# Two of six down groups of each FFN as seven half-size products, and low parts of weights made by adding transfers

## The chip, the cores and the metric

The kernel runs on one core of a Trainium2 chip. Its engines work side by side, each from its own queue in order: TensorE (PE: matmuls into PSUM, with its weight loads, PEld, beside them), VectorE (DVE), ScalarE (ACT), GpSimd (POOL) and SyncE (SP, which only starts transfers). Sixteen DMA engines move data for all of them. The metric is device microseconds of one execution of the whole program; lower is better.

## The reference

A decoder trunk of two layers on x of 1 x 512 x 1024 in float32. Each layer is a half-step SwiGLU FFN, a mixer (gated linear attention in the first layer, stick-breaking attention in the second), and another half-step FFN; a norm ends the trunk. So there are four FFNs, and they hold most of the work:

```python
def swiglu(h, w_gate, w_up, w_down):
    return (jax.nn.silu(h @ w_gate) * (h @ w_up)) @ w_down
...
for i in range(DEPTH):
    x = x + 0.5 * swiglu(rmsnorm(x, ffn1_norm[i]), ffn1_w_gate[i], ffn1_w_up[i], ffn1_w_down[i])
    h = rmsnorm(x, mix_norm[i])
    ...
    x = x + y.astype(x.dtype)
    x = x + 0.5 * swiglu(rmsnorm(x, ffn2_norm[i]), ffn2_w_gate[i], ffn2_w_up[i], ffn2_w_down[i])
```

The model width is 1024, the hidden width 2816, the sequence 512 tokens.

## The kernel before, in words

**Tiling.** Everything is held transposed: features on the 128 partitions, the 512 tokens along the free dimension. x is eight tiles of 128 x 512 (`xs`). A float32 product is made of three matmuls in a shorter format (`F32R`): each operand is cut into a high part h (the value cast on ACT) and a low part l = value - h (a subtraction on DVE), and the matmuls are h h, l h and h l. `Entry.split` (lines 110 to 135) cuts weights, `FFN.cut` (668) cuts activations.

**Order of the work.** All weight products stand in one list, `feed.q`. An `Entry` has one or two units of weights (a unit is at most 128 x 1024 elements of a loaded chunk, or sums made from it) and a body that issues its matmuls. `Feed.start` (141) begins an entry: it splits the units of this entry and of the next two, as long as they hold at most four full units together, makes the views (the sums) of the next four and loads the chunks of the next six. Four buffers of high and of low parts (`wh`, `wl`) go round, so a unit can be cut when the matmuls of the unit four places earlier are through. Loads are started by SyncE in order, each when its buffer is free: two buffers of 1 MB (`raw`) and two of 512 KB (`rawd`, for down weights). The framework's planner orders each engine's queue from the program's order, its own costs and the dependencies.

**One FFN.** The 11 blocks of 256 hidden features form six groups, `GROUPS = ((0, 2), (2, 4), (4, 6), (6, 8), (8, 9), (9, 11))`. Gate and up of the first two blocks are plain products (`feat`: 24 matmuls of 512 columns each); all others use `seven` (560): the product of a 2 x 2 block matrix by seven products of half size in place of eight (Strassen's scheme in Winograd's form), with 12 matmuls of 256 columns for each. Sums of weights are made on DVE (`sums_12`, `sums_34`), sums of the activations once per FFN (`sums`). A seven is two entries: the first block column and s12 (`body_1`, four products), s34 and a half unit a22 (`body_2`, three products). `gate` and `close` turn the result into hidden tiles (h, l) of 128 x 512.

The down products of a group are `down` entries (297), placed between the sevens of the next group: for a group of two blocks (four hidden tiles) four entries, each with 24 matmuls of 512 columns into two PSUM tiles `ps_d`, which DVE then adds into x (323). The last group's downs end the FFN; in the last FFN `back_tok` takes their place. Where a seven follows an entry whose weights lie at another offset, a copy of its first 128 x 128 weights is made as well (`lead`, 131 to 135).

PSUM has eight banks of 128 x 512 that `psum` hands out in turn.

Of the kernel before, what the change touches and what calls it, by code (L numbers as in the profile page):

```python
# [28 lines left out]
NEAR, NEAR_MOVING = 16, 48  # L29
# [3 lines left out]
def decoder(ctx: ExitStack, tc: tile.TileContext, a: dict, out: bass.AP):  # L33
    nc = tc.nc
# [60 lines left out]
    class Entry:  # L95
# [3 lines left out]

        def __init__(self, units, body, place=0, lead=False):  # L100
            self.units, self.body, self.W, self.place = units, body, None, place
            self.lead, self.views = lead, None

        def view(self):

# [1 line left out]
                self.views = [view(ch.load()) for ch, view, _, _ in self.units]  # L107
            return self.views

        def split(self):  # L110
            if self.W is None:
                self.W = []
                for r, (_, _, n, m) in zip(self.view(), self.units):
                    few = n * m < 1024
                    if few:

                        h = st["few"].tile([P, n * m + NEAR], F32R, tag="vh", bufs=1, name="wh")[:, NEAR:]
                        l = st["few"].tile([P, n * m + 64 - NEAR], F32R, tag="vl", bufs=1, name="wl")[:, : n * m]
                    else:
                        h, l = (  # L120
                            wp.tile([P, n * m + 64], F32R, tag="w" + t, bufs=4, name="w" + t)[
                                :, self.place : self.place + n * m
                            ]
                            for t in "hl"
                        )
                    h, l = (t.rearrange("p (n m) -> p n m", m=m) for t in (h, l))
                    st["cut"] = nc.scalar.copy(h, r).ins  # L127
                    with tc.issue_after(st["gains"]):
                        nc.vector.tensor_tensor(out=l, in0=r, in1=h.bitcast(F32), op=ALU.subtract)  # L129
                    self.W.append((h, l))  # L130
                    if self.lead and len(self.W) == 1:

                        first = wp.tile([P, m], F32R, tag="w1", bufs=1, name="w1")
                        nc.scalar.copy(first, r[:, 0])
                        self.first = first

    class Feed:
# [46 lines left out]
    feed = Feed()  # L184
# [112 lines left out]
    def down(w, r0, nf, hs, part, nxt, late=0):  # L297


        nd = KD // nf  # L300
        src = w[r0 : r0 + nf * P, part * nd * P : (part + 1) * nd * P]
        ch = Chunk(src.rearrange("(f p) c -> p f c", p=P), nf, nd * P)
        ch.few = True

        def body(W):
            (wh, wl), = W
            acc = []

            def prod(m, fs):
                if m == len(acc):  # L310
                    acc.append(psum("ps_d"))
                s = slice(m * P, (m + 1) * P)
                for f in fs:
                    mm3(acc[m], wh[:, f, s], wl[:, f, s], hs[f][0], hs[f][1], f == 0, f == nf - 1)

            if late:
                for m in range(nd):
                    prod(m, range(nf - late))
            for m in range(nd):
                prod(m, range(nf - late if late else 0, nf))  # L320
                ps = acc[m]
                k = part * nd + m
                nc.vector.scalar_tensor_tensor(  # L323
                    out=xs[k], in0=ps, scalar=0.5, in1=xs[k], op0=ALU.mult, op1=ALU.add
                )
                if nxt is not None:
                    nxt(k)
                yield

        feed.q.append(Entry([(ch, lambda t: t, nf, nd * P)], body))  # L330

    def back_tok(w, r0, nf, hs, done):

# [159 lines left out]
    class FFN:  # L493
# [5 lines left out]

        GROUPS = ((0, 2), (2, 4), (4, 6), (6, 8), (8, 9), (9, 11))  # L500
        NORMED, SEVEN, AHEAD = 6, 2, 2
        SEVEN_UP = (2, 3, 4, 5, 6, 7, 8, 9, 10)

        def __init__(self, wg, wu, wd, gi, nxt, first=False, last=False):
            self.gi, self.normed = gi, False
            self.after_ffn = bool(phases) and isinstance(phases[-1], FFN)
            self.defer, self.gates = [], []
            self.lead = []
            self.hs = [[] for _ in self.GROUPS]
            base, downs = len(feed.q), []  # L510
# [48 lines left out]

        def seven(self, ch, group=None):  # L560
# [62 lines left out]
            def body_2(W):  # L623
# [9 lines left out]
                nc.vector.tensor_tensor(out=o0[:, H:T], in0=q, in1=o0[:, H:T], op=ALU.add)  # L633
                gate(o0, H, o0[:, H:T])
                if group is not None:
                    self.close(o0, group)
                gate(o1, H, o1[:, H:T])
                yield
                prod(w, a22, 0, lambda j: self.t_half(3, j), first=False)
                gate(o1, 0, w)  # L640
                if group is not None:
                    self.close(o1, group)
                    del self.gates[:2]
                else:
                    self.gates += [o0, o1]
                yield


            lead = feed.q[-1].place != NEAR
# [70 lines left out]
        def close(self, t, group):  # L720
            h = self.hp.tile([P, T], F32R, tag="hh", name="hh")
            l = self.hp.tile([P, T], F32R, tag="hl", name="hl")
            self.hs[group].append(self.cut(h, l, t))

        def run(self, between=None):
            with tc.tile_pool(name="hp", bufs=8, reuse_waits="tile") as self.hp, tc.tile_pool(
# [712 lines left out]
```

## Time and profile before

| | us |
|---|---|
| median of 3 runs (1855.47 to 1856.14) | 1856.08 |
| the profiled execution | 1854.57 |
| its span, first to last instruction | 1852.6 |
| PE busy in it | 1836.5 (99%) |
| DVE busy | 1421.5 (77%) |
| ACT busy | 1012.7 (55%) |
| POOL busy | 8.8 |
| mean granted TensorE clock | 0.999 |

A group's row gives line, engine, operation, output<-inputs, shape and count, then the busy time in us with the mean ns of one instruction, then the idle time of the engine before them and what ended it. In the table of waits a row says who waited, for whom, the total in us, how often, and the longest. In the chain, a row is start, length and engine with tile and line, xN for N instructions in a row. PE's matmuls overlap, so the duration of one is longer than the distance from one to the next.

### The profile page before, as it was taken

The numbers are of one execution on the slowest core, as the hardware profiler recorded it, in microseconds if no ns is written. First come the engines' busy times: TensorE is split into PE (matmuls) and PEld (weight loads), VectorE is DVE, ScalarE is ACT, GpSimd is POOL, SyncE is SP. The second block draws the span as 40 slices with busy tenths as digits, with TensorE's granted clock in tenths as the row PEclk, the third lists the DMA queues.
The fourth block names the chain that finished last, engine by engine and source line by source line (L and its number), as shares of the span: only waits on it lengthen the run. The fifth ranks groups of instructions, "written<-read, shape, count | busy, mean of one in ns | idle before, by whom it ended". The sixth has DMA issues, their size and how long they took to land.

```text
span 1852.6 us, 29092 instructions
## 1 busy us (share of the span) xinstructions
PE 1836.5 (99%) x11899; PEld 1645.3 (89%) x11899; DVE 1421.5 (77%) x2172; ACT 1012.7 (55%) x1735; POOL 8.8 (0%) x20
## 2 busy tenths in 40 slices
PE   8999999999999999999999999999999999999998
PEld 7999999889888899999889999998878788999997
DVE  7977776776787987777798777676878779877775
ACT  7545545444555554544555545455888755544454
POOL 0000000100000000000000000000000000000000
PEclk9999999999999999999999999999999999999999
DMA  5333333221223233333233333222221123333321
GB/s 160 114 126 114 103 115 102 91 68 48 69 69 114 91 114 108 109 103 102 85 111 114 103 103 114 98 86 80 69 69 61 65 91 97 120 103 110 119 80 69
DMA packets 177610, 179.11 MB, mean 97 GB/s; under 512 B 4099, under 2 KB 167989, under 8 KB 177477
## 3 DMA queue, kind: packets, MB, share of 16 engines
q1 hardware_dynamic: 176768, 176.18, 29.5%
q8 instruction: 93, 1.52, 0.3%
q0 software_dynamic: 608, 1.05, 0.2%
q14 instruction: 41, 0.33, 0.1%
q10 hardware_dynamic: 100, 0.03, 0.0%
HBM read 175.17 MB, written 2.10 MB: 96 GB/s over the span
## 4 chain that ended last, share of the span: by engine, by line
PE 95%; DVE 2%; ACT 2%; DMA 1%; issue 0%; SPq 0%; ACTq 0%; DVEq 0%
PE ps_d L67 25%; PE ps_w L587 21%; PE ps_f L67 18%; PE ps_q L587 10%; PE ps_z L587 5%; PE ps_t L67 5%; PE ps_b L67 4%; PE ps_S L67 1%; PE ps_bt L67 1%; PE ps_z L1163 1%; PE ps_oT L1225 1%; PE ps_T L1210 1%; PE ps_o L67 1%; DMA x<-in_x_dram 1%; ACT wh L127 0%; DVE wl L129 0%
## 5 line engine op out<-in xcount | busy, mean ns | idle before, releaser
L129 DVE TENSOR_TENSOR wl<-raw,wh 128x1024 fp32r<-128x1024 f32 (+1 forms) x244 | 258.8, 1063 | 91.8 <-ACT wh L127 59.7
L127 ACT CAST wh<-raw 128x1024 fp32r<-128x1024 f32 (+1 forms) x244 | 224.8, 923 | 119.3 <-PE ps_d L67 40.1
L67 PE MATMUL ps_d<-hh,wl 128*128 128x512 f32 x672 | 262.1, 390 | 0.0
L67 PE MATMUL ps_d<-hh,wh 128*128 128x512 f32 x672 | 262.1, 390 | 0.0
L67 PE MATMUL ps_d<-hl,wh 128*128 128x512 f32 x672 | 261.4, 389 | 0.0
L587 PE MATMUL ps_w<-th,wh 128*128 128x256 f32 x864 | 238.8, 276 | 0.4 <-ACT ps_z L611 0.4
L587 PE MATMUL ps_w<-tl,wh 128*128 128x256 f32 x864 | 238.6, 276 | 0.0
L587 PE MATMUL ps_w<-th,wl 128*128 128x256 f32 x864 | 238.5, 276 | 0.0
L127 ACT CAST wh<-s 128x1024 fp32r<-128x1024 f32 x144 | 151.1, 1049 | 121.0 <-PE ps_q L587 41.5
L129 DVE TENSOR_TENSOR wl<-s,wh 128x1024 fp32r<-128x1024 f32 x144 | 175.6, 1221 | 51.4 <-PE ps_z L587 28.3
L323 DVE SCALAR_TENSOR_TENSOR x<-ps_d,x 128x512 f32<-128x512 f32 x184 | 124.7, 687 | 101.3 <-PE ps_d L67 100.4
L127 ACT CAST wh<-rawd 128x1024 fp32r<-128x1024 f32 x84 | 88.5, 1055 | 179.7 <-PE ps_d L67 97.3
L67 PE MATMUL ps_f<-xh,wh 128*128 128x512 f32 x448 | 179.0, 400 | 0.0
L67 PE MATMUL ps_f<-xl,wh 128*128 128x512 f32 x448 | 175.7, 392 | 0.0
L67 PE MATMUL ps_f<-xh,wl 128*128 128x512 f32 x448 | 175.1, 391 | 0.0
L587 PEld LDWEIGHTS ps_w<-th,wh 128*128 128x128 f32 x864 | 162.2, 188 | 0.8 <-ACT ps_z L611 0.8
L587 PEld LDWEIGHTS ps_w<-th,wl 128*128 128x128 f32 x864 | 162.2, 188 | 0.0
L587 PEld LDWEIGHTS ps_w<-tl,wh 128*128 128x128 f32 x864 | 162.2, 188 | 0.0
L67 PEld LDWEIGHTS ps_d<-hl,wh 128*128 128x128 f32 x672 | 126.2, 188 | 26.7
L67 PEld LDWEIGHTS ps_d<-hh,wh 128*128 128x128 f32 x672 | 126.1, 188 | 24.7
L67 PEld LDWEIGHTS ps_d<-hh,wl 128*128 128x128 f32 x672 | 126.1, 188 | 24.1
L129 DVE TENSOR_TENSOR wl<-rawd,wh 128x1024 fp32r<-128x1024 f32 x84 | 102.8, 1224 | 52.9 <-ACT wh L127 39.1
(276 smaller groups left out, 4442.2 us busy)
## 6 DMA issues: line engine op xcount, KB each, us to landing
raw<-in_ffn_w_gate_dram SPq DMA_DIRECT2D x43, 1024.0 KB, 5.1
raw<-in_ffn_w_up_dram SPq DMA_DIRECT2D x43, 1024.0 KB, 5.2
rawd<-in_ffn_w_down_dram SPq DMA_DIRECT2D x84, 512.0 KB, 3.5
raw<-in_gla_w_in_dram SPq DMA_DIRECT2D x12, 1024.0 KB, 5.5
raw<-in_sb_w_in_dram SPq DMA_DIRECT2D x16, 512.0 KB, 3.8
raw<-in_gla_w_out_dram SPq DMA_DIRECT2D x4, 1024.0 KB, 4.9
raw<-in_sb_w_in_dram SPq DMA_DIRECT2D x4, 1024.0 KB, 5.3
raw<-in_sb_w_out_dram SPq DMA_DIRECT2D x4, 1024.0 KB, 4.9
```

Of the source, the lines that this page charges most:

```text
L67: st["pe"] = nc.tensor.matmul(ps, l, r, start=first, stop=last).ins
L127: st["cut"] = nc.scalar.copy(h, r).ins
L129: nc.vector.tensor_tensor(out=l, in0=r, in1=h.bitcast(F32), op=ALU.subtract)
L323: nc.vector.scalar_tensor_tensor(out=xs[k], in0=ps, scalar=0.5, in1=xs[k], op0=ALU.mult, op1=ALU.add)
L587: st["pe"] = nc.tensor.matmul(o, l_, r_, start=first and j + n == 0, stop=j == 3 and n == 2, skip_group_check=True).ins
L1163: nc.tensor.matmul(o_, l_, r_, start=first, stop=last, skip_group_check=True)
L1210: nc.tensor.transpose(ps[:, c0 : c0 + P], ys[yb][:, yc + j * P : yc + (j + 1) * P], ident)
L1225: nc.tensor.matmul(po[e * 64 : e * 64 + 64, j * P : T], self.v[j][:, c : c + 64], self.wt[p, e][bk][:, c0 : c0 + n], start=j == 0, stop=j ...
```

## The change

Three things change.

First, the down products of the second and the fourth group (`DOWN_SEVEN = (1, 3)`) are no longer four `down` entries each but two parts of a new function, `seven_down`: the same seven-product scheme with the down weights as the left matrix (two chunks of 512 KB, `lower` and `upper`, in the two `rawd` buffers) and the hidden tiles as the right one. A part makes four of the eight output tiles. It uses six PSUM banks; ACT copies two of them from bank to bank, and each product is added by DVE into half a tile of x as soon as it stands. Part 0 comes after the second seven of the next group, part 1 after the first seven of the group behind that.

Second, the hidden tiles of those groups are closed in another form: `close_first` and `close_second` make the sums of the right matrix (four differences of 128 x 256 on DVE) and cut them and the plain quarters. Their high and low parts lie in the hidden tiles' buffers, in halves of the normed input that no product reads then, and in two tiles of the norm.

Third, the low part of some units is no longer made by a DVE subtraction: ACT writes l = -value in the short format, and GpSimd starts a transfer that adds the loaded value to it. This holds for the first unit of every entry with `adds`: plain `down` entries, sevens that are no `lead`, and the first entry of each `seven_down` part. `Feed.start` gains a rule that splits the first unit of such an entry one entry earlier. As a side effect fewer sevens follow a plain down, so fewer have `lead`.

```diff
@@ class Entry @@
+    def split(self, few=None):
+
         if self.W is None:
             self.W = []
-            for r, (_, _, n, m) in zip(self.view(), self.units):
+        if len(self.W) < len(self.units):
+            for r, (_, _, n, m) in list(zip(self.view(), self.units))[len(self.W) : few]:
...
                 st["cut"] = nc.scalar.copy(h, r).ins
+                if self.adds and len(self.W) == 0:
+
+                    nc.scalar.activation(l, r, AF.Copy, scale=-1.0)
+                    nc.gpsimd.dma_start(out=l, in_=r, accum_op=ALU.add)
+                    self.W.append((h, l))
+                    continue
...
@@ Feed.start @@
             if used > 4:
+
+                if used == 5 and len(e.units) == 2 and e.adds:
+                    e.split(1)
                 break
...
+    def seven_down(pool, w, r0, hs, part):
...
+        H = T // 2
+        lower, upper = (
+            Chunk(w[r0 : r0 + 4 * P, c : c + 256].rearrange("(f p) c -> p f c", p=P), 4, 256)
+            for c in (part * 256, 512 + part * 256)
+        )
+        lower.few = upper.few = True
...
+        def sums_12(_):
+            a11, _, a21, a22 = halves()
+            s = v["s12"] = pool().tile([P, 4, 256], F32, tag="s", bufs=4, name="s12")
+            nc.vector.tensor_tensor(out=s[:, 0:2], in0=a21, in1=a22, op=ALU.add)
+            nc.vector.tensor_tensor(out=s[:, 2:4], in0=s[:, 0:2], in1=a11, op=ALU.subtract)
+            return s
...
+        def prod(ps, w, k0, step, m, b, first):
+            for c in range(2):
+                bh, bl = hs[c][b]
+                wh, wl = (t[:, k0 + step * c, m * P : (m + 1) * P] for t in w)
+                for n, (l_, r_) in enumerate(((wh, bh), (wl, bh), (wh, bl))):
+                    st["pe"] = nc.tensor.matmul(
+                        ps, l_, r_, start=first and c + n == 0, stop=c == 1 and n == 2, skip_group_check=True
+                    ).ins
+
+        def add(m, up, col, ps):
+            x = xs[part * 2 + m + 4 * up][:, col * H : col * H + H]
+            nc.vector.scalar_tensor_tensor(out=x, in0=ps, scalar=0.5, in1=x, op0=ALU.mult, op1=ALU.add)
+
+        def body_1(W):
+            ax, s = W
+            ws, zs, qs = [], [], []
+            for m in range(2):
+                ws.append(psum("ps_w")[:, 0:H])
+                prod(ws[m], ax, 0, 2, m, "b11", True)
+            for m in range(2):
+
+
+                zs.append(psum("ps_z")[:, 0:H])
+                nc.scalar.copy(zs[m], ws[m])
+            yield
+            for m in range(2):
+                qs.append(psum("ps_q")[:, 0:H])
+                prod(qs[m], s, 0, 1, m, "t1", True)
+                add(m, 1, 1, qs[m])
+            yield
...
+        def body_2(W):
+            s, a22 = W
+            ws, qs = v["w"], v["q"]
+            for m in range(2):
+                prod(ws[m], s, 0, 1, m, "t3", False)
+                add(m, 1, 1, ws[m])
+            yield
...
+        feed.q.append(
+            Entry([(lower, lambda t: t, 4, 256), (lower, sums_12, 4, 256)], body_1, NEAR, feed.q[-1].place != NEAR)
+        )
+        assert not feed.q[-1].lead
+        feed.q[-1].adds = True
+        feed.q.append(Entry([(lower, sums_34, 4, 256), (upper, lambda t: halves()[3], 2, 256)], body_2, NEAR))
...
@@ class FFN @@
+    DOWN_SEVEN = (1, 3)
...
+                if late and i == 0:
+                    seven_down(*late.pop())
                 while c >= self.SEVEN and put < len(downs) * (i + 1) // slots:
                     down(*downs[put])
                     put += 1
+                if group - 1 in self.DOWN_SEVEN and i == 1:
+                    args = (lambda: self.tp, wd, self.GROUPS[group - 1][0] * 256, self.hs[group - 1])
+                    seven_down(*args, 0)
+                    late.append((*args, 1))
...
+            if group in self.DOWN_SEVEN:
+                downs = []
...
+        entry.adds = not lead
...
+    def close_first(self, o0, group):
...
+        n, H = len(self.hs[group]), T // 2
+        h, l = (self.n[n][i][:, H:T] for i in range(2))
+        self.hs[group].append({"b11": self.cut(h, l, o0[:, 0:H])})
+
+    def close_second(self, o0, o1, group):
+
+        b, H = self.hs[group][-1], T // 2
+        ts = self.tp.tile([P, 4, H], F32, tag="s", bufs=4, name="ts")
+
+        def sub(i, p, q):
+            nc.vector.tensor_tensor(out=ts[:, i], in0=p, in1=q, op=ALU.subtract)
+
+        sub(0, o0[:, H:T], o0[:, 0:H])
+        sub(1, o1[:, H:T], ts[:, 0])
+        sub(2, o1[:, H:T], o0[:, H:T])
+        sub(3, o1[:, 0:H], ts[:, 1])
...
+        h, l = self.cut(*two(), o1)
+        b["b21"], b["b22"] = (h[:, 0:H], l[:, 0:H]), (h[:, H:T], l[:, H:T])
+        h, l = self.cut(*two(), ts[:, 0:2].rearrange("p a b -> p (a b)"))
+        b["t1"], b["t2"] = (h[:, 0:H], l[:, 0:H]), (h[:, H:T], l[:, H:T])
...
```

More of the change, by code (lines that the diff above doesn't have):

```diff
@@ L131, in split @@
                     if self.lead and len(self.W) == 1:
-                        first = wp.tile([P, m], F32R, tag="w1", bufs=1, name="w1")
-                        nc.scalar.copy(first, r[:, 0])
+                        first = wp.tile([P, P], F32R, tag="w1", bufs=1, name="w1")
+                        nc.scalar.copy(first, r[:, 0, 0:P])
                         self.first = first
@@ L330, in down, with halves, sums_34 @@
         feed.q.append(Entry([(ch, lambda t: t, nf, nd * P)], body))
+        feed.q[-1].adds = True
[6 more added lines that the diff above has]
+        lower.few = upper.few = True
+        v = {}
+        def halves():
+            lo, up = (c.load().rearrange("p (c two) d -> p two c d", two=2) for c in (lower, upper))
+            return lo[:, 0], lo[:, 1], up[:, 0], up[:, 1]
+        def sums_12(_):
[4 more added lines that the diff above has]
+            return s
+        def sums_34(_):
+            a11, a12, a21, _ = halves()
+            s = pool().tile([P, 4, 256], F32, tag="s", bufs=4, name="s34")
+            nc.vector.tensor_tensor(out=s[:, 0:2], in0=a11, in1=a21, op=ALU.subtract)
+            nc.vector.tensor_tensor(out=s[:, 2:4], in0=a12, in1=v["s12"][:, 2:4], op=ALU.subtract)
+            return s
+        def prod(ps, w, k0, step, m, b, first):
[25 more added lines that the diff above has]
+            for m in range(2):
+                prod(ws[m], s, 2, 1, m, "t2", False)
+                add(m, 0, 1, ws[m])
+            yield
+            for m in range(2):
+                prod(zs[m], ax, 1, 2, m, "b21", False)
+                add(m, 0, 0, zs[m])
+            v["w"], v["q"] = ws, qs
+            yield
+        def body_2(W):
+            s, a22 = W
+            ws, qs = v["w"], v["q"]
+            for m in range(2):
+                prod(ws[m], s, 0, 1, m, "t3", False)
+                add(m, 1, 1, ws[m])
+            yield
+            for m in range(2):
+                prod(qs[m], s, 2, 1, m, "b22", False)
+                add(m, 0, 1, qs[m])
+            yield
+            for m in range(2):
+                prod(ws[m], a22, 0, 1, m, "t4", False)
+                add(m, 1, 0, ws[m])
+            yield
+        feed.q.append(
+            Entry([(lower, lambda t: t, 4, 256), (lower, sums_12, 4, 256)], body_1, NEAR, feed.q[-1].place != NEAR)
+        )
+        assert not feed.q[-1].lead
+        feed.q[-1].adds = True
+        feed.q.append(Entry([(lower, sums_34, 4, 256), (upper, lambda t: halves()[3], 2, 256)], body_2, NEAR))
@@ L509, in __init__ @@
             self.hs = [[] for _ in self.GROUPS]
-            base, downs = len(feed.q), []
+            base, downs, late = len(feed.q), [], []
             self.sums_by = 10**6
@@ L723, in close, with two @@
             self.hs[group].append(self.cut(h, l, t))
+        def close_first(self, o0, group):
[11 more added lines that the diff above has]
+            sub(3, o1[:, 0:H], ts[:, 1])
+            def two():
+                return (self.hp.tile([P, T], F32R, tag=t, name=t) for t in ("hh", "hl"))
+            h, l = self.cut(*two(), o1)
+            b["b21"], b["b22"] = (h[:, 0:H], l[:, 0:H]), (h[:, H:T], l[:, H:T])
+            h, l = self.cut(*two(), ts[:, 0:2].rearrange("p a b -> p (a b)"))
+            b["t1"], b["t2"] = (h[:, 0:H], l[:, 0:H]), (h[:, H:T], l[:, H:T])
+            if len(self.hs[group]) == 1:
+                for i in (2, 3):
+                    h, l = (t[:, H:T] for t in self.n[i])
+                    b[f"t{i + 1}"] = self.cut(h, l, ts[:, i])
+            else:
+                h = sp.tile([P, T], F32R, tag="sq", name="t34")
+                l = sp.tile([P, T], F32R, tag="ss", name="t34")
+                self.cut(h, l, ts[:, 2:4].rearrange("p a b -> p (a b)"))
+                b["t3"], b["t4"] = (h[:, 0:H], l[:, 0:H]), (h[:, H:T], l[:, H:T])
         def run(self, between=None):
```

17 lines of the change are left out of this document (13 added, 4 removed).

## The prediction

> **What bounds the kernel now.** I read the page first, then the waits of TensorE, then the chain that ended last. The page says which engine is full and how loaded the helpers are:
>
> ```profile
> span 1852.6 us, 29092 instructions
> PE 1836.5 (99%) x11899; PEld 1645.3 (89%) x11899; DVE 1421.5 (77%) x2172; ACT 1012.7 (55%) x1735; POOL 8.8 (0%) x20
> ...
> q1 hardware_dynamic: 176768, 176.18, 29.5%
> ...
> PE 95%; DVE 2%; ACT 2%; DMA 1%; issue 0%; SPq 0%; ACTq 0%; DVEq 0%
> ```
>
> The reader sees 99% of the span on PE, and a chain that is PE for 95%. A busy share alone could hide waits, so the waits of PE come next; their whole list is this:
>
> ```profile
> PE ps_g L1360 <- DMA gl<-in_gla_o_norm_dram: 6.5, 1, 6.5
> PE ps_x L1367 <- DMA x<-in_x_dram: 0.9, 2, 0.7
> PE ps_oT L1225 <- ACT wt L490: 0.6, 2, 0.4
> PE ps_w L587 <- ACT ps_z L611: 0.4, 2, 0.2
> PE ps_z L1163 <- DVE r L1196: 0.2, 1, 0.2
> ```
>
> After the start (6.5 and 0.9 us for the input) PE waits 1.2 us in all. So the time is the sum of PE's instructions at their pitch, and one matmul fewer is time saved as long as nothing new makes PE wait. DVE, ACT and the DMA engines matter only where they come late.
>
> **What PE gives up.** The mean duration of a matmul (390 ns for 512 columns, 276 ns for 256) can't be used, since matmuls overlap; the chain shows the pitch. Its pieces in the last stages of the first FFN:
>
> ```profile
> 239.90 1.36 PE ps_w L587 x12
> ...
> 249.42 10.90 PE ps_d L67 x48
> ...
> 299.80 5.46 PE ps_d L67 x24
> ```
>
> Twelve matmuls of 256 columns take 1.36 us (113 ns each); 48 of 512 columns take 10.90 us (227 ns). Two of the first cost one of the second, so half size has no penalty here. A group of four features goes down in four entries of 24 matmuls of 512: 2 x 10.90 = 21.8 us. After the change it is two parts of seven products; a product is 2 x 2 x 3 = 12 matmuls of 256, one step of 1.36 us, so 14 x 1.36 = 19.0 us. That is 2.8 us less per group; two groups in each of four FFNs: 8 x 2.76 = 22.1 us less on PE. The adding transfers change nothing on PE.
>
> **What is added beside PE.** These group rows, shapes kept apart, give the prices:
>
> ```profile
> L129 DVE TENSOR_TENSOR wl<-raw,wh 128x1024 fp32r<-128x1024 f32 x172 | 209.8, 1221 | 88.2 <-ACT wh L127 56.1 <-PE ps_z L587 30.8
> L323 DVE SCALAR_TENSOR_TENSOR x<-ps_d,x 128x512 f32<-128x512 f32 x184 | 124.7, 687 | 101.3 <-PE ps_d L67 100.4
> L570 DVE TENSOR_TENSOR s<-raw 128x512 f32<-128x512 f32 x72 | 49.5, 687 | 7.9 <-DMA raw<-in_ffn_w_gate_dram 4.2 <-DMA raw<-in_ffn_w_up_dram 3.4
> L600 DVE TENSOR_TENSOR o<-ps_z,o 128x256 f32<-128x256 f32 x36 | 15.0, 417 | 0.0
> ...
> L127 ACT CAST wh<-rawd 128x1024 fp32r<-128x1024 f32 x84 | 88.5, 1055 | 179.7 <-PE ps_d L67 97.3 <-issue 69.8 <-PE ps_q L587 9.5
> L669 ACT CAST hh<-o 128x512 fp32r<-128x512 f32 x72 | 43.9, 621 | 39.4 <-DVE o L600 39.4
> L134 ACT CAST w<-raw 128x128 fp32r<-128x128 f32 x56 | 16.4, 292 | 2.9 <-DMA raw<-in_ffn_w_up_dram 2.9
> L611 ACT COPY ps_z<-ps_w 128x256 f32<-128x256 f32 x72 | 25.8, 358 | 7.6 <-PE ps_w L587 4.2
> ```
>
> DVE, per FFN. Closing a pair of hidden tiles for the new form: four differences of 256 columns (4 x 0.42) and cuts of 0.42 + 0.69 + 0.69 + 0.8 in place of 2 x 0.69, so +2.85, for four pairs +11.4. One part of a new down: four weight sums (4 x 0.69), low parts 2 x 1.22 + 0.69, twelve adds of 256 columns into x (12 x 0.42 = 5.0): 10.9, four parts 43.5; the eight plain entries that go cost 1.22 + 2 x 0.69 = 2.6 each, 20.8; so +22.7. Off DVE go low parts that a transfer now makes, 1.22 each: in the order of the queue these are 14 plain downs (10 in the last FFN) and 10 first units of sevens per FFN: -29.3 (the four first units of parts are made by transfers too, but DVE never had them). Net +4.8 per FFN, +9.7 in the last, +24 us over the run: 1445 of some 1835, 79%. ACT: cuts +4, parts 4 x (3 x 1.06 + 0.61 + 2 x 0.36) - 8 x 1.06 = +9.5, negations 28 x 1.06 = +30, six leading 128-column casts fewer (-1.8), +41 per FFN and +161 in all: 1174, 64%. Averages have room; the question is the thick stretch.
>
> The thickest is the eighth gate to the ninth up with both parts of the fourth group among them (six entries of 9.52 us PE = 57 us). DVE there by durations: gate 7.9, up 9.7, part 10.9, gate 6.7, part 10.9, up 9.7 = 55.8 us, 98%. Durations overlap, though. Windows of before, two of which are those stages:
>
> ```profile
> 18.00:60.00 42.00, 42.00 (x189) 34.41 (x189) 40.60 (x74) 28.17 (x43) 0.00 (x0) 1.00 0.41 131
> ...
> 240.00:280.80 40.80, 40.80 (x266) 37.02 (x265) 29.88 (x43) 17.08 (x28) 0.00 (x0) 1.00 0.35 118
> 280.80:324.30 43.50, 43.50 (x361) 42.54 (x360) 29.03 (x42) 24.44 (x43) 0.00 (x0) 1.00 0.34 109
> ```
>
> The columns are PE, PEld, DVE, ACT, POOL, clock, DMA share, GB/s. DVE goes from 73 and 67% here towards 85 to 98%. The first row says what that costs: DVE busy 40.60 of 42 us, PE 42.00 of 42. So a nearly full DVE need not hold PE. The part has one tight exchange, two copies PSUM to PSUM of 0.36 us on ACT before PE returns to the same bank; the seven has the same with one copy and lost 0.4 us in 72 of them (the wait row above). Bounds for 16 parts: 0 us, and one cast of 1.06 us late each, 17 us. I take 0.25 us each, 4 us, near the row of the seven.
>
> **The adding transfers.** 108 low parts (28 per FFN, 24 in the last) come from: cast, negation on ACT, issue on POOL, transfer, semaphore. Only their lateness can cost. The window of a plain down, in the order of time (ACT, then DVE, then SyncE):
>
> ```profile
> 105.06 1.05 ACT L127 CAST wh<-rawd 128x1024 fp32r<-128x1024 f32 x1 [3.26 <-PE ps_d L67]
> 106.42 0.36 ACT L611 COPY ps_z<-ps_w 128x256 f32<-128x256 f32 x1
> ```
>
> ```profile
> 106.14 1.23 DVE L129 TENSOR_TENSOR wl<-rawd,wh 128x1024 fp32r<-128x1024 f32 x1 [0.39 <-ACT wh L127]
> 108.25 0.69 DVE L570 TENSOR_TENSOR s<-raw 128x512 f32<-128x512 f32 x1 [0.88 <-DMA raw<-in_ffn_w_up_dram]
> ```
>
> ```profile
> 102.93 0.37 SPq L92 DMA_DIRECT2D raw<-in_ffn_w_up_dram  x1
> 107.40 0.37 SPq L92 DMA_DIRECT2D rawd<-in_ffn_w_down_dram  x1
> 117.51 0.37 SPq L92 DMA_DIRECT2D raw<-in_ffn_w_gate_dram  x1
> ```
>
> The cast starts when the previous down leaves the buffer, four units back; the next down starts one seven later, 7 x 1.36 = 9.5 us, and its second matmul is the first to read the low part. Cast and negation take 2.1 us, a copy of 0.36 us may come between, so the transfer has about 7 us from issue to landing. The low part that was ready at 107.4 will be ready near 112. The buffer of the raw down weights comes free that much later: SyncE's next load waits 5 us more, but the load queued behind it goes at 117.5, so nothing is pushed; that load's own cast comes two sevens and two downs on, 30 us after this one. For first units of sevens the window is as long: their buffer is that of a sum unit two entries back, and the new half-entry split exists to start them one entry early. What a transfer costs, from issues of before:
>
> ```profile
> raw<-in_ffn_w_up_dram SPq DMA_DIRECT2D x43, 1024.0 KB, 5.2
> ...
> fin<-in_final_norm_dram POOLq DMA_DIRECT2D x1, 512.0 KB, 4.0
> ...
> gr<-in_gla_w_in_dram POOLq DMA_DIRECT2D x1, 64.0 KB, 3.9
> tri<-in_c_tri_dram POOLq DMA_DIRECT2D x1, 64.0 KB, 2.0
> ```
>
> ```profile
> 324.50 1.04 POOL L824 DMA_DIRECT2D gr<-in_gla_w_in_dram  x1 [323.20 <-DVE o L600]
> ...
> 1788.67 0.53 POOL L1291 DMA_DIRECT2D fin<-in_final_norm_dram  x1 [550.83 <-DVE wl L129]
> ```
>
> No row shows an add. Lower bound: a plain transfer of that size from POOL, 4.0 us. Upper: three passes (source, target, write) at q1's price, 0.295 x 1852.6 us over 176.18 MB, 1.6 us per 512 KB on 16 engines: 2.0 + 3 x 1.6 = 6.8, the extra POOL time of pieces (1.04 - 0.53 = 0.5, the first units are cut in pieces of 512 bytes), and a weight load sharing the engines (3.2 us): 10.5 us. I take 5.5 us, the 1 MB load plus half of the piecing, as it is nearest to twice the bytes: below 7, nothing on PE. The upper end is 3.5 us late. A gain below nothing is excluded, since PE does not wait for low parts now. POOL's queue holds only these transfers and a dozen small ones; SyncE, ACT and DVE are not queued behind them.
>
> **Sum.** Against the profiled 1854.57 us (its span 1852.6 and 2 us around it; 1.5 below the median 1856.08): 1854.6 - 22.1 + 4 = 1836.5, and as a median of runs 1838, from which I take off nothing: 1838 us, 1.0% faster.
>
> **Rivals.**
> The adds land late (the other side). Place: second matmul of each unit made by a transfer. Price: the lateness times 108. It decides from 18 / 108 = 0.17 us mean lateness upwards, that is from transfers of about 7.2 us; at 0.5 us late it is 1838 + 54 = 1892, at 0.3 us 1870. For it: loads and adds meet on the same engines, DMA share 0.35 in these windows, and an add's rate is unknown. Against: the price above, and 7 us of window.
>
> DVE holds PE in the thick stretches. Place: fifth and sixth group of each FFN, and the third. If PE must wait for what DVE lacks at 98% and in order, 2 us in each of 8 groups: 1838 + 16 = 1854 at the worst end, 1846 in the middle. For it: 55.8 of 57 us. Against: the 42 us window at 97%.
>
> Descriptor writing is locked out by DVE. The 42 us window above leaves DVE 1.4 us free, so a POOL that had to wait for DVE to pause could lose several us per add; with half of the adds 6 us late: 1838 + 54 x 6 = 2160 us. The Trainium skill, SBUF — State Buffer, section "SBUF: two separate sides", says this of transfers issued from GpSimd while VectorE runs an operation in its two-port mode, an fp32 copy from SBUF to SBUF for one; its section "Who interferes with whom" takes tensor_tensor out of it. By that rule the sum stays, since the rows here are TENSOR_TENSOR and SCALAR_TENSOR_TENSOR; no run here has shown it for adding transfers.
>
> The change buys nothing: a saving eaten to within noise, 1852 to 1860.
>
> **Chances and range.** Forecast (1829 to 1843) 0.50; DVE holds PE (1843 to 1852) 0.13; within 0.2% (3.7 us, about what a measurement can tell) 0.05; adds late 0.29; lock-out 0.03. Faster 0.63, same 0.05, slower 0.32. For 8 in 10 the range must reach into late adds: 1829 to 1872, which leaves out most of the 0.32 above 0.3 us lateness (0.17) and little below. The forecast's own range is 1829 to 1843.
>
> **What the profile will show.** Right: PE still near 99%, ps_d at 672 - 256 = 416 of each of its three kinds, 1344 new 256-column matmuls at 113 ns pitch, PE's list of waits under 15 us, DVE about 1445 us, ACT about 1174 us, 108 POOL transfers of 512 KB landing in 4 to 7 us. Wrong: PE rows that wait for a DMA of wl (adds late), for DVE x or wl (DVE), or landings over 7 us. Most likely to break it: an add that moves far slower than a plain transfer.

## The result, and the profile after

| | before | after |
|---|---|---|
| median, us | 1856.11 | 1949.1 (1943.37 to 1952.2) |
| profiled execution, us | 1854.57 | 1949.29 |
| its span, us | 1852.6 | 1947.5 |
| PE busy, us | 1836.5 | 1860.1 |
| PE idle (span less busy), us | 16.1 | 87.4 |
| mean granted clock | 0.999 | 0.982 |

The changed kernel is 5% slower: the ratio is 1.050, interval 1.0487 to 1.0513. The forecast was 1838 us, and its range ended at 1872.

The page of the changed kernel, its first lines, the DMA queues and the shares of the chain:

```profile
span 1947.5 us, 31041 instructions
PE 1860.1 (96%) x12475; PEld 1686.9 (87%) x12475; DVE 1418.8 (73%) x2392; ACT 1155.1 (59%) x1923; POOL 130.8 (7%) x128
...
q1 hardware_dynamic: 176768, 176.18, 28.4%
q0 software_dynamic: 52000, 57.68, 20.4%
...
PE 63%; DVE 14%; DMA 13%; issue 5%; ACT 4%; SPq 0%; DVEq 0%; ACTq 0%; POOLq 0%; POOL 0%
```

PE has fallen from 95% of the chain to 63%, and DMA has risen from 1% to 13%. DVE did not get busier (1421.5 us before). PE is still busy for 96%, part of it at half clock (below), but it no longer makes the time alone: instructions wait for each other. PE's waits of the changed kernel, the longest totals:

```profile
PE ps_w L702 <- ACT u L744: 25.0, 10, 3.5
...
PE ps_w L380 <- DVE x L386: 21.3, 11, 6.2
...
PE ps_w L702 <- ACT ps_z L726: 8.8, 8, 2.1
PE ps_d L67 <- DMA wl<-rawd: 6.0, 5, 2.2
```

The reader is to see what is *not* at the top. The row for a low part that landed late, `wl<-rawd`, has 6.0 us. PE waits far more for small helpers, a copy on ACT and an add on DVE, which are not late by their own work. What stands ahead of them shows in the order of time. First ACT (left: start and duration; in brackets: idle time before, and what ended it):

```profile
87.21 2.14 ACT L129 CAST wh<-s 128x1024 fp32r<-128x1024 f32 x2
93.01 0.30 ACT L142 CAST w<-raw 128x128 fp32r<-128x128 f32 x1 [3.66 <-DMA raw<-in_ffn_w_up_dram]
93.22 0.37 ACT L744 COPY u<-ps_w 128x256 f32<-128x256 f32 x1
```

ACT stands still for 3.66 us at a lead cast of the *next* seven, whose load has not landed. The copy that the *running* seven needs is behind it in the queue, and PE starts again only at 93.64:

```profile
93.64 0.38 PE L702 MATMUL ps_w<-th,wh 128*128 128x256 f32 x1 [2.65 <-ACT u L744]
```

Why the load was late is in the transfers of the changed kernel between 78 and 96 us (queues, then issues with us to landing):

```profile
q0 software_dynamic: 1724, 0.87, 44.8%
q1 hardware_dynamic: 1040, 1.05, 18.6%
...
raw<-in_ffn_w_up_dram SPq DMA_DIRECT2D x1, 1024.0 KB, 8.7
wl<-raw POOLq DMA_DIRECT2D x1, 512.0 KB, 8.8
```

POOL and SyncE issued them shortly after each other:

```profile
82.75 1.54 POOL L133 DMA_DIRECT2D wl<-raw  x1 [6.70 <-ACT wl L132]
```

```profile
84.33 0.37 SPq L92 DMA_DIRECT2D raw<-in_ffn_w_up_dram  x1
```

They share the 16 DMA engines, and the load took 8.7 us instead of the usual 5.2. Before the change, a load met no such traffic.

The same happens on DVE in a part of the fourth group:

```profile
276.19 0.95 DVE L386 SCALAR_TENSOR_TENSOR x<-ps_w,x 128x256 f32<-128x256 f32 x2
281.25 0.69 DVE L364 TENSOR_TENSOR s<-rawd 128x512 f32<-128x512 f32 x1 [4.11 <-DMA rawd<-in_ffn_w_down_dram]
281.87 0.75 DVE L386 SCALAR_TENSOR_TENSOR x<-ps_z,x 128x256 f32<-128x256 f32 x2
282.53 2.35 DVE L137 TENSOR_TENSOR wl<-s,wh 128x1024 fp32r<-128x1024 f32 x2
284.80 0.69 DVE L365 TENSOR_TENSOR s<-s,rawd 128x512 f32<-128x512 f32 x1
285.40 0.75 DVE L386 SCALAR_TENSOR_TENSOR x<-ps_w,x 128x256 f32<-128x256 f32 x2
```

A sum waits 4.11 us for down weights. Their load was issued two microseconds after an add, and landed 6.8 us later in place of the usual 3.5:

```profile
272.52 1.57 POOL L133 DMA_DIRECT2D wl<-raw  x1 [9.35 <-DVE o L715]
```

```profile
274.43 0.37 SPq L92 DMA_DIRECT2D rawd<-in_ffn_w_down_dram  x1
```

Behind the sum stand the adds into x that let PE go back to the same bank; in this stretch PE waited once, for such an add:

```profile
PE ps_w L380 <- DVE x L386: 5.1, 1, 5.1
```


A stall costs PE a second time. Stretches of the changed kernel around the stall at 93 us, and right after the one that ended at 178.6 (columns: PE, PEld, DVE, ACT, POOL busy, granted clock, DMA share, GB/s):

```profile
90.00:94.00 4.00, 1.35 (x12) 1.16 (x11) 1.37 (x3) 0.99 (x4) 0.00 (x0) 1.00 0.54 171
94.80:98.20 3.40, 3.40 (x19) 3.40 (x18) 3.16 (x9) 2.37 (x6) 0.88 (x1) 0.50 0.49 95
98.20:100.00 1.80, 1.80 (x17) 1.80 (x17) 1.28 (x4) 1.51 (x4) 0.00 (x0) 0.99 1.00 147
...
180.10:183.50 3.40, 3.40 (x19) 3.40 (x18) 3.40 (x8) 2.25 (x5) 0.59 (x1) 0.51 0.74 134
```

The second stall's own row:

```profile
178.59 0.39 PE L702 MATMUL ps_w<-th,wh 128*128 128x256 f32 x1 [1.91 <-ACT u L744]
```

Some 1.2 us after the stall of 2.65 us ended, PE's clock falls to 0.50 for 3.4 us. The stall of 1.91 us had the same sequel, 1.6 us after its end. The trace's clock records put all 15 such falls of this kernel on one raster of 3.41 us. In the window of the raster just before a fall PE was idle for 1.85 us or more; of the windows that full clock followed, none after the first 7 us had over 1.80 us of idle time. So in this trace what counts is the idle time within such a window, and a little over half of it is enough. Over the run the mean clock of 0.982 makes (1 - 0.982) x 1947.5 = 35 us. The Trainium skill, "TensorE: Matmul & The Clock Gate", section "Part 1: The HAM clock gate", says that the array falls to half clock after one idle window of about 3.4 us. The 3.4 us at half clock agree with that length; the stalls that led to it were shorter here, and the measurement decides.

**Where the 95 us are.** PE's sum by the forecast's first step would give busy 1836.5 - 22.1 = 1814.4 and, with the old 16.1 us of idle, a span of 1830.5. Measured: busy 1860.1 (+46: up to 33 us of it is the half clock, 35 less the 2 that a mean of 0.999 makes before; the rest is a longer pitch in places) and idle 87.4 (+71). Together +117; less the 22 saved, 95 us, the growth of the span. The table in the last experiments splits every variant in this way.

### The profile page after: what moved, and what is told of

Its sections match the earlier page's. It is cut to its first block, busy times and chain, and to the rows that moved or that the text cites. A ratio compares the mean times of both kernels' runs of the same rounds, so it can differ in the third digit from the quotient of the medians.

```text
span 1947.5 us, 31041 instructions
## 1 busy us (share of the span) xinstructions
PE 1860.1 (96%) x12475; PEld 1686.9 (87%) x12475; DVE 1418.8 (73%) x2392; ACT 1155.1 (59%) x1923; POOL 130.8 (7%) x128
## 3 DMA queue, kind: packets, MB, share of 16 engines
q1 hardware_dynamic: 176768, 176.18, 28.4%
q8 instruction: 97, 1.59, 0.3%
## 4 chain that ended last, share of the span: by engine, by line
PE 63%; DVE 14%; DMA 13%; issue 5%; ACT 4%; SPq 0%; DVEq 0%; ACTq 0%; POOLq 0%; POOL 0%
PE ps_w L702 13%; PE ps_f L67 12%; PE ps_d L67 10%; PE ps_q L702 6%; DMA raw<-in_ffn_w_up_dram 5%; PE ps_t L67 4%; DVE wl L137 4%; PE ps_b L67 4%; PE ps_z L702 3%; PE ps_w L380 3%; DMA wl<-rawd 3%; DMA raw<-in_ffn_w_gate_dram 3%; DMA rawd<-in_ffn_w_down_dram 3%; ACT wh L129 2%; PE ps_S L67 1%
## 5 line engine op out<-in xcount | busy, mean ns | idle before, releaser
L137 DVE TENSOR_TENSOR wl<-raw,wh 128x1024 fp32r<-128x1024 f32 (+1 forms) x204 | 211.1, 1035 | 137.6 <-PE ps_z L702 68.9
L137 DVE TENSOR_TENSOR wl<-s,wh 128x1024 fp32r<-128x1024 f32 x176 | 214.3, 1221 | 95.9 <-PE ps_z L702 61.4
L67 PE MATMUL ps_d<-hh,wl 128*128 128x512 f32 x416 | 163.7, 393 | 6.2 <-DMA wl<-rawd 6.0
L67 PE MATMUL ps_d<-hh,wh 128*128 128x512 f32 x416 | 162.9, 392 | 0.0
L67 PE MATMUL ps_d<-hl,wh 128*128 128x512 f32 x416 | 162.6, 391 | 0.0
L133 POOL DMA_DIRECT2D wl<-rawd x68 | 59.5, 875 | 1279.4 <-ACT wl L132 719.8
L132 ACT ACTIVATE wl<-rawd 128x1024 fp32r<-128x1024 f32 x68 | 71.7, 1060 | 91.0 <-PE ps_d L67 50.6
L334 DVE SCALAR_TENSOR_TENSOR x<-ps_d,x 128x512 f32<-128x512 f32 x120 | 80.5, 690 | 34.1 <-PE ps_d L67 34.0
L67 PEld LDWEIGHTS ps_f<-xl,wh 128*128 128x128 f32 x448 | 84.5, 189 | 19.1 <-DVE xl L486 1.0
L67 PEld LDWEIGHTS ps_f<-xh,wh 128*128 128x128 f32 x448 | 84.8, 190 | 17.5 <-ACT xh L485 1.2
```

Of the source, the lines that this page charges most:

```text
L67: st["pe"] = nc.tensor.matmul(ps, l, r, start=first, stop=last).ins
L132: nc.scalar.activation(l, r, AF.Copy, scale=-1.0)
L133: nc.gpsimd.dma_start(out=l, in_=r, accum_op=ALU.add)
L334: nc.vector.scalar_tensor_tensor(out=xs[k], in0=ps, scalar=0.5, in1=xs[k], op0=ALU.mult, op1=ALU.add)
```

## The experiments

Theory A: the seven-product downs save PE time as forecast, and the adding transfers, through the loads that they disturb, lose it and more. Theory B: the seven-product downs themselves hold PE, with their tight exchanges between PE, ACT and DVE, and the transfers are a side matter.

### The halves of the change

All low parts by DVE again, the seven-product downs kept:

```diff
-        feed.q[-1].adds = True
...
-        feed.q[-1].adds = True
...
-            entry.adds = not lead
```

> The seven-product down alone: every low part by DVE again. Theory A (adding transfers hold the buffers of raw weights and share the DMA engines, so weight loads land late, ACT and DVE block in order behind them, PE stalls and its clock drops): the saving of 22 us shows, 1834 to 1850 us. Theory B (the seven-product down itself, its PSUM exchanges and its adds into x, makes PE wait): 1890 us or more.

Measured: 1856.47 us, ratio 1.0006 (0.9996 to 1.0016). Neither theory had that. Taking the adding transfers away wins back all of the loss, so B is wrong for it; but nothing is left of the 22 us either, so A is wrong about the saving.

The transfers alone, with all downs plain:

```diff
-        DOWN_SEVEN = (1, 3)
+        DOWN_SEVEN = ()
```

> The adding transfers alone: all down groups plain again, 84 plain downs and 16 first units of sevens made by transfers. Theory A: slower than before, 1870 to 1930 us. Theory B: 1850 to 1860 us.

Measured: 1894.25 us, ratio 1.0214 (1.0199 to 1.0229). The transfers cost 39 us also where no seven-product down exists. The same wait leads the list of this kernel as in the changed one:

```profile
PE ps_w L702 <- ACT u L744: 13.2, 5, 3.0
```

Transfers for down weights only (plain entries and parts), and for plain entries only:

```diff
-            entry.adds = not lead
```

> As the changed kernel, but first units of sevens by DVE; transfers only from the 512 KB buffers (52 plain downs, 16 parts). Theory A, if the 1 MB buffers are the ones that matter: 1845 to 1880 us. Theory A, if those of 512 KB matter as much: 1890 to 1920. Theory B: within 10 us of 1949.

```diff
             Entry([(lower, lambda t: t, 4, 256), (lower, sums_12, 4, 256)], body_1, NEAR, feed.q[-1].place != NEAR)
...
-        feed.q[-1].adds = True
...
-            entry.adds = not lead
```

> As the changed kernel, but transfers only for the 52 plain downs; parts and sevens by DVE. Theory A: 1838 to 1865 us, below the run that has them for the parts too. Theory B: within 15 us of 1949.

Measured: 1887.59 (ratio 1.0173, 1.0156 to 1.0190) and 1878.73 (1.0126, 1.0111 to 1.0141). Both miss the ranges of theory A: the first lies between its two, the second 14 us above its one. The ranges supposed the saving of 22 us, which is not there even without the adds. From none to all, in steps: the 52 adds of plain downs cost 1878.73 - 1856.47 = 22 us, the 16 of the parts 9 us more, the 40 of the sevens 1949.1 - 1887.59 = 61.5 us more: 0.43, 0.55 and 1.54 us for each. The last are the ones from the 1 MB buffers `raw`, moved in pieces of 512 bytes. The order of the steps is one of several; what each kind would cost alone was not run.

### What eats the 22 us

The kernel without adding transfers spends its 22 us in the parts. Its longest wait of PE in the changed places, then DVE in the order of time in the fourth group:

```profile
PE ps_w L379 <- DVE x L385: 10.8, 16, 1.4
```

```profile
267.36 1.22 DVE L137 TENSOR_TENSOR wl<-s,wh 128x1024 fp32r<-128x1024 f32 x1
268.49 0.68 DVE L363 TENSOR_TENSOR s<-rawd 128x512 f32<-128x512 f32 x1
269.10 0.41 DVE L385 SCALAR_TENSOR_TENSOR x<-ps_w,x 128x256 f32<-128x256 f32 x1
```

The add that frees a bank (L385) stands in DVE's queue behind a low part and a weight sum for later entries, and PE waits 10.8 us at 16 such places. The rest of the 22 us is not in this row: three shorter waits in the parts make 3.0 us (`ps_q` for DVE 1.5 and for ACT 1.0, `ps_w` for ACT's copy 0.5). But the starts of the matmuls in the trace lie some 22 us further apart in the parts than at the pitch of before, waits included, so the remainder passes for busy time. Three edits followed. The first leaves out the weight sums of `seven_down`, the second gives them to POOL, the third lets ACT copy the two banks out that PE returns to (each twice in a part), so that DVE adds from the copy whenever it comes to it:

```diff
         def sums_12(_):
-            a11, _, a21, a22 = halves()
-            ...
-            return s
+            halves()
+            return upper.load()
...
         def sums_34(_):
-            ...
+            return lower.load()
```

> The seven-product down with all low parts by DVE, without its weight sums: the 64 sums of 128 x 512 are left out and the loaded chunks stand in their place, so the output is not the reference's. It takes 64 x 0.6 = 38 us off DVE and nothing off PE. If DVE eats the saving (its stretches beside the parts are full): 1834 to 1845 us. If PSUM exchanges or the order do: 1850 to 1857 us.

```diff
-            nc.vector.tensor_tensor(out=s[:, 0:2], in0=a21, in1=a22, op=ALU.add)
+            nc.gpsimd.tensor_tensor(out=s[:, 0:2], in0=a21, in1=a22, op=ALU.add)
...
```

> The seven-product down with all low parts by DVE, its 64 weight sums on GpSimd. If DVE eats the saving and GpSimd does not hold DVE up: 1836 to 1850 us, better than the kernel before. If the two share a way to SBUF, or GpSimd takes several us per sum: 1856 us or more.

```diff
-        def add(m, up, col, ps):
+        def add(m, up, col, ps, out=False):
...
+            if out:
+                u = pool().tile([P, H], F32, tag="c", bufs=2, name="u")
+                nc.scalar.copy(u, ps)
+                ps = u
...
-                add(m, 0, 1, ws[m])
+                add(m, 0, 1, ws[m], True)
...
-                add(m, 1, 1, ws[m])
+                add(m, 1, 1, ws[m], True)
...
-                u3 = self.tp.tile([P, H], F32, tag="c", bufs=1, name="u3")
+                u3 = self.tp.tile([P, H], F32, tag="c", bufs=2, name="u3")
```

> The seven-product down with all low parts by DVE, and in its parts the bank that is written again (after t2 and after t3) is first copied to SBUF by ACT, as the sevens do, and DVE adds from the copy; PE then waits for ACT and not for DVE. If PE's wait for the DVE adds is what is left of the loss (16 us of gaps in the run without adding transfers): 1838 to 1848 us, better than the kernel before. If ACT is as late in its queue as DVE: 1852 to 1860 us.

All three stand on the kernel without adding transfers (1856.47). Measured: without sums 1849.84 (ratio to before 0.9971, 0.9960 to 0.9982), a gain of 6.6 us on it; sums on POOL 1891.91 (1.0192, 1.0175 to 1.0209), a loss of 35; banks copied out **1846.81** (0.9954, 0.9940 to 0.9967), a gain of 9.7. The first falls at the edge of the second range expected, the second into its bad range, the third into its good one. So it is less the amount of DVE's work than the place of the freeing add in its queue: 64 sums fewer win no more than 64 copies on ACT, which take nothing off DVE (1529.9 us busy against 1531.7). The last one beats the kernel before by 8 us, 0.5%. Its edit also gives the sevens a second buffer for their copy `u`; that alone was not run, but PE's wait for that copy did not fall by it (1.5 us before, 1.8 after). In PE's list of waits no `ps_w` waits for `DVE x` any more (one `ps_q` of a seven does, 2.2 us), and in the stretch that the forecast called the thickest (first row: without adding transfers; second: banks copied out besides) PE fills up while DVE stays as full as it was:

```profile
240.00:280.80 40.80, 40.02 (x343) 39.39 (x343) 39.65 (x65) 23.36 (x40) 0.00 (x0) 1.00 0.36 117
```

```profile
240.00:280.80 40.80, 40.73 (x359) 40.53 (x358) 39.66 (x66) 26.17 (x49) 0.00 (x0) 1.00 0.35 113
```

Sums on POOL fail by their price and by what they do to DVE. One of the four groups of them, and a sum for the sevens that stays on DVE:

```profile
L370 POOL TENSOR_TENSOR s<-rawd 128x512 f32<-128x512 f32 x16 | 28.1, 1754 | 35.0 <-DVE t L795 22.7 <-issue 7.7 <-DVE wl L137 4.6
```

```profile
L690 DVE TENSOR_TENSOR s<-raw,s 128x512 f32<-128x512 f32 x72 | 62.5, 869 | 0.3
```

A sum takes 1.46 to 1.75 us there (means of the four groups) in place of 0.69 on DVE. And DVE is held up beside it: the 60 sums of L690 that meet no sum on POOL take 0.69 us, the 12 that do take up to 1.78. DVE's 2436 instructions are busy for 1545.0 us, against 1492.2 for as many in the run without the sums. That is how the expectation's "the two share a way to SBUF" would show; its "several us per sum" did not come.

### What an adding transfer costs, apart from being late

Here the low parts come from DVE, so no product can wait for a transfer, and transfers of the same size and number run beside them: 108 that add the cast tile to a scratch in HBM (the rule that splits a first unit early is off).

```diff
-                    if self.adds and len(self.W) == 0:
-                        ...
                     with tc.issue_after(st["gains"]):
                         nc.vector.tensor_tensor(out=l, in0=r, in1=h.bitcast(F32), op=ALU.subtract)
+                    if self.adds and len(self.W) == 0:
+                        ...
+                        nc.gpsimd.dma_start(out=j, in_=h.bitcast(F32), accum_op=ALU.add)
```

> The seven-product down with all low parts by DVE, and beside it 108 transfers that nobody waits for: the size, the pieces and the adding of the changed kernel, but read from the high part and written to HBM, so that no raw buffer is held. If the engines they take from the weight loads are the price of the adding transfers: 1890 us or more. If holding the raw buffers is the price: 1856 to 1866 us.

Next, no traffic, but the raw buffer held about as long, by a chain of three small transfers whose last one reads it:

```diff
+                        a_, b_ = st["junk"]
+                        nc.gpsimd.dma_start(out=a_, in_=h[:, 0, 0:16].bitcast(F32))
+                        nc.gpsimd.dma_start(out=b_, in_=a_)
+                        nc.gpsimd.dma_start(out=b_, in_=r[:, 0, 0:16], accum_op=ALU.add)
```

> The seven-product down with all low parts by DVE, and beside it, for the same 108 units, a chain of three transfers of 64 bytes per partition, the last of which reads the raw buffer, so that the buffer is held some 6 to 7 us after the cast with next to no traffic. If holding is the price: 1900 to 1950 us. If traffic is the price: 1856 to 1866 us.

Both at once were meant with the traffic read from the raw buffer itself, and then, since that moved the start of the transfers, with the traffic of the first and a small transfer behind it that reads the raw buffer:

```diff
-                        nc.gpsimd.dma_start(out=j, in_=h.bitcast(F32), accum_op=ALU.add)
+                        nc.gpsimd.dma_start(out=j, in_=r, accum_op=ALU.add)
```

> As the run with 108 transfers to HBM that nobody waits for, but read from the raw buffer, so that they take engine time and hold the buffer as the changed kernel's do. If the two prices add up: 1856 + 50 + 11 = 1917 us. If they feed each other: 1930 us or more, and little of the changed kernel's 1949 is left for the adds' own lateness. If holding costs nothing beside the traffic: 1906 us.

```diff
                         nc.gpsimd.dma_start(out=j, in_=h.bitcast(F32), accum_op=ALU.add)
+                        nc.gpsimd.dma_start(out=j[:, 0, 0:16], in_=r[:, 0, 0:16], accum_op=ALU.add)
```

> As the run with 108 transfers to HBM read from the high part (they start after the cast, when the next weight load is due), and behind each a transfer of 64 bytes per partition that reads the raw buffer, so that the buffer is held until the large one has landed and some 2 us more. If collision and holding add up: 1906 + 11 = 1917 us. If they feed each other: 1930 to 1950 us. If holding is nothing beside the collision: 1906 us.

Measured, with PE's busy and idle time against the 1814.4 and 16.1 us of the forecast's sum (profiled executions):

| kernel | median, us | ratio to before (interval) | on the kernel without adds | PE busy | PE idle |
|---|---|---|---|---|---|
| banks copied out, no adds | 1846.81 | 0.9954 (0.9940 to 0.9967) | -10 | +4 | +7 |
| no adds | 1856.47 | 1.0006 (0.9996 to 1.0016) | 0 | +10 | +15 |
| early traffic | 1864.46 | 1.0052 (1.0039 to 1.0066) | +8 | +15 | +19 |
| hold | 1867.25 | 1.0065 (1.0050 to 1.0080) | +11 | +16 | +21 |
| traffic | 1906.21 | 1.0277 (1.0261 to 1.0292) | +50 | +28 | +46 |
| traffic and hold | 1931.82 | 1.0408 (1.0385 to 1.0431) | +75 | +41 | +60 |
| the change | 1949.1 | 1.050 (1.0487 to 1.0513) | +93 | +46 | +71 |

Traffic that nobody waits for costs 50 us; holding with next to no traffic costs 11, just past the range expected if traffic is the price. The landings show how the traffic does it; first the kernel without adding transfers, then with the traffic:

```profile
raw<-in_ffn_w_up_dram SPq DMA_DIRECT2D x43, 1024.0 KB, 5.6
rawd<-in_ffn_w_down_dram SPq DMA_DIRECT2D x84, 512.0 KB, 3.5
```

```profile
junk<-wh POOLq DMA_DIRECT2D x108, 512.0 KB, 6.0
...
raw<-in_ffn_w_up_dram SPq DMA_DIRECT2D x43, 1024.0 KB, 7.0
rawd<-in_ffn_w_down_dram SPq DMA_DIRECT2D x84, 512.0 KB, 5.7
```

These weight loads land 1.4 and 2.2 us later (those of the gate hardly, 5.3 against 5.2), and PE's waits are those of the changed kernel again:

```profile
PE ps_w L704 <- ACT u L746: 13.2, 10, 3.1
PE ps_w L384 <- DVE x L390: 12.7, 16, 2.9
```

The early traffic was a miss, and the most telling run. Its bytes and their share of the engines are the same (21.4% on its queue, 21.0% with the later traffic), yet it costs 8 us in place of 50. Its transfers begin when the raw buffer has landed. The later ones begin when the cast is done, about when DVE too is through with the buffer and SyncE loads again: at one place the transfer at 175.25 us and the loads at 177.56 and 178.16; with the early traffic a load at 150.71, the transfer at 156.39 and the next load at 160.83. So the early ones lie between the loads, and these land nearly as without traffic:

```profile
junk<-rawd POOLq DMA_DIRECT2D x68, 512.0 KB, 5.8
...
raw<-in_ffn_w_up_dram SPq DMA_DIRECT2D x43, 1024.0 KB, 5.7
rawd<-in_ffn_w_down_dram SPq DMA_DIRECT2D x84, 512.0 KB, 3.6
```

The two runs differ in one thing more, the buffer that the transfers read (`wh`, and raw in the early run), but ACT, which writes `wh` again, has no wait for such a transfer in its list. So the price is not the load on the DMA engines as a whole but the meeting of an add with a load that is needed soon. The early traffic held the raw buffers hardly at all (SyncE waited for these transfers 51.5 us in all), which is why the last run was made. There, hold and traffic together cost 75 us, in the range expected if they feed each other and more than 50 + 11. It is not that held-back loads meet more adds: the down loads landed in 3.7 us there, against 5.7 with the traffic alone. They start late: at its casts of down weights ACT waited 65.3 us for them, against 21.5 with the traffic and 27.8 with the hold. How much of the 75 us this makes was not measured. SyncE's waits in the changed kernel show both kinds of hold; before the change SyncE waited for no such transfer:

```profile
SPq L92 <- DMA wl<-raw: 282.1, 40, 16.1
SPq L92 <- DMA wl<-rawd: 276.1, 57, 9.5
```

From 75 to the 93 us of the change 17 are left. PE's own waits for a late low part (6.0 us) are among them; the rest, possibly the planner's other order with the negations on ACT and the early split, was not taken apart and stays open. The split into traffic and hold is also a likeness: the scratch lies in HBM, while the change adds into SBUF, and none of these runs has the 113 us (1531.7 - 1418.8) by which the change relieves DVE.

## Why the prediction was wrong

**PE's sum was right.** `ps_d` has 416 matmuls of each of its three kinds, as forecast, and the chain of the changed kernel has the parts' steps at the forecast pitch in places and a little above in others, here two steps of one part and one of a later part:

```profile
146.48 1.41 PE ps_w L380 x12
147.90 1.41 PE ps_q L380 x12
...
740.55 1.36 PE ps_w L380 x12
```

That the saving is real shows with the banks copied out, where 8 of the 22 us reach the clock on the wall.

**The helpers' totals were right and did not matter.** DVE 1418.8 us (1445 forecast), ACT 1155.1 (1174).

**The exchanges of the 16 parts were mis-sized.** The step "I take 0.25 us each, 4 us" came from the wait of a seven, whose exchange is one copy on ACT. In a part, the bank comes free by DVE's add, and that add stands behind work for later entries in the same queue. Without adding transfers the parts lost all of the 22 us, above the forecast's upper bound of 17 us and its rival's 16 us. The reading "a nearly full DVE need not hold PE" was right of the stretch it came from, and right again with the banks copied out; it does not carry over to a place where PE waits for one certain instruction of the full engine.

**The step that failed is the one on the adding transfers**, and in it two sentences. "Only their lateness can cost": PE's waits for late low parts are 6.0 us of the 93. "SyncE's next load waits 5 us more, but the load queued behind it goes at 117.5, so nothing is pushed": that was read from one place of the trace, for one kind of unit; the profile after has 97 waits of SyncE for an add, up to 16.1 us. With it fell "SyncE, ACT and DVE are not queued behind them". The runs put in its place: 50 us for the traffic beside the loads, 75 us with the raw buffers held as well, of the 93 us. The size of the landing was not the mistake:

```profile
wl<-rawd POOLq DMA_DIRECT2D x68, 512.0 KB, 5.1
wl<-raw POOLq DMA_DIRECT2D x40, 512.0 KB, 7.2
```

5.1 us for whole rows is below the 5.5 taken; 7.2 us for pieces of 512 bytes is in the bounds, and at the 7 us of the window. The bound of 10.5 us even held "a weight load sharing the engines", but as a price of the add. What the load itself loses by the sharing, and who stands behind that load in ACT's and DVE's queues, was not asked.

**The rivals.** "The adds land late" had the sign (1892 us at half a microsecond of lateness, against 1949.1 measured), but named the wrong place: the second matmul of a unit, where only 6.0 us are lost. "DVE holds PE" was right of the parts and priced too low. A lock-out of descriptor writing did not show: POOL took 0.88 us per issue from `rawd` and 1.57 from `raw`, none of the 108 took over 0.99 and 1.59, and 5.1 us is 1.1 above the plain transfer from POOL that the forecast showed. "PE's list of waits under 15 us" was the line of the forecast that showed the mistake at first sight: the first row alone has 25.0.

## What to carry to other kernels

A transfer that takes work off an engine is paid for by the loads that it meets or holds back: place it by the times at which loads must start, and ask what each later load holds up. An in-order queue makes a late load everybody's delay, so an instruction that waits for a load of the next entry should not stand ahead of one that frees a bank for the running entry; a copy out of PSUM on the engine with room is a cheap way to uncouple them. And read a wait for its place in the queue: an engine's mean load says little about when it reaches the one instruction that PE needs.

## What the runs showed of the hardware that was not expected

An adding transfer of 512 KB occupies all 16 DMA engines for 0.204 x 1947.5 / 108 = 3.7 us, against 1.6 us (0.284 x 1947.5 over 176.18 MB) for as many plain bytes from HBM, and it lands in 5.1 us in rows of 4 KB and 7.2 us in pieces of 512 bytes, with the issue on POOL growing from 0.88 to 1.57 us. Not all of that is the pieces': in the early traffic, which lies between the loads and goes to HBM, the two landed in 5.8 and 6.2 us. Transfers of the same number, size and pieces cost 8 us or 50 us by the time at which they start. A sum on DVE with both inputs in SBUF took up to 1.78 us in place of 0.69 while POOL made sums. And PE's clock fell to 0.50 for 3.4 us after stalls of 1.91 and 2.65 us.
